# The convolution module of a decoder trunk: where the norm, the output weights and the layer norm stand in the queues

## The chip, the cores and the metric

The kernel runs on one core of one Trainium2 chip. Its engines each work through a queue of their own in order: TensorE (PE) multiplies matrices, VectorE (DVE) and GpSimd (POOL) do elementwise work and reductions, ScalarE (ACT) activations and copies, SyncE (SP) issues most of the transfers. The metric is the device time of one execution in microseconds (us). It is 1263.67 us before, the median of three runs (1261.9 to 1269.88).

## What is computed

Two decoder layers over 512 positions with 1024 channels, in float32. Each layer is a mixer and a SwiGLU feed-forward network, both behind an RMS norm and added to the residual. The mixer of layer 0 is a convolution module, that of layer 1 is sparse attention. What the change names is the convolution module:

```python
def conformer_conv_module(h, w_in, b_in, w_dw, b_dw, ln_g, ln_b, w_out):
    a, g = jnp.split(h @ w_in + b_in, 2, axis=-1)
    u = a * jax.nn.sigmoid(g)
    u = lax.conv_general_dilated(u, w_dw[:, None, :], (1,), padding=[(CONV_WIDTH - 1, 0)], ...) + b_dw
    mu = jnp.mean(u, axis=-1, keepdims=True)
    var = jnp.mean(jnp.square(u - mu), axis=-1, keepdims=True)
    u = (u - mu) * lax.rsqrt(var + LN_EPS) * ln_g + ln_b
    return jax.nn.silu(u) @ w_out
```

Its input h is rmsnorm(x), the convolution runs over 31 positions, each channel for itself. The attention projects h to queries, keys, values and gates; queries and keys are each normalized per head and rotated in part of their channels (rope):

```python
    q = partial_rope(rmsnorm(q, q_gain), positions)
    k = partial_rope(rmsnorm(kv[:, 0], k_gain[:, None, None, None, :]), positions)
```

## The kernel before

All activations lie with channels on the 128 partitions and the 512 positions along them, so x is 8 chunks of 128 x 512. Every product with a weight is made of three matmuls: the weight tile wr is split into a rounded part wh (ScalarE, L198) and the rest wl = wr - wh (VectorE, L207), the input into hh and hl in the same way, and mm3 (L258 to L260) adds wh x hh, wh x hl and wl x hh. Weight tiles come in a fixed sequence: w_dma (L183) issues the load of a tile on SP, next_w (L210) splits a tile, starts the split of the next and loads up to four ahead. proj_tile (L356) makes one 128 x 512 result of 24 matmuls. After its fourth input chunk it splits the next wl and calls `mid`, if one was given. proj_start (L333) makes the first four results of a projection together, chunk by chunk of the input.

The order on each engine is partly set by a scheduler: instructions given to tc.keep_in_program_order keep their place in the written order, `after(a, b)` puts a behind b, and the others are placed by the scheduler. mm3 pins its matmuls only while a flag (`hold`) is set.

The convolution module (L370) goes through these steps. The input projection starts with the raw x, and the norm's scale R comes later: norm_a (L314) sums the squares (ssq) and runs a chain of small operations for the inverse root, norm_b (L323) spreads the scale over all partitions (rbc, eight matmuls) and copies it to Rb. glu(i) (L416) then makes gr and ar (a result times Rb) and u_i from the two results pA and pG of chunk i. A loop (L599) makes pA and pG of chunk i, with glu of chunk i - 1 between them. Chunks 0 and 1 are convolved on VectorE (cv, L438), chunks 2 to 7 on PE: conv_pe_load stores u_i to memory in one layout (swap<-u, L451) and loads it in another (uf<-swap, L452), conv_pe multiplies it with a band matrix (cpe, L471), adds bias terms (L475), stores (swap<-uf, L476) and loads it back (u<-swap, L481). The sums for the layer norm of a PE chunk are the matmuls lng (ph_sum, L519). The table CONV_AT says at which chunk of the loop each of these steps is written down: "c" a convolution, "g" the sums of one, "w" the loads, "n" and "m" the sums of chunks 0 and 1, "t" the spreading of these (lnrt). Three buffers hold uf, so the sixth and later loads wait until an older chunk's sums are done.

ln_rows (L544) makes the two rows rs and mr of the layer norm, spread by lnb. ln_out(i) (L618) normalizes a chunk: a product and a subtraction on VectorE (L621 or L623, L624), two activations (L630) and the low part (L631). proj_start calls it one chunk ahead of the output projection, whose eight chunks need weight tiles wr18 to wr25. Tiles 18 to 20 are loaded in the loop before `at(8)`.

In the attention layer (layer 1), q_tiles (L1410) makes the query results, six of them through proj_tile with `mid` set to a function that runs the steps of the table MIDS and may be empty; the keys' results and the first two of the queries', ahead of them, give no `mid`. Between the tiles stand short pieces of PE work: qk_rs (L997) sums the squares of a group of heads (psq), turns them (qat), takes the inverse root on VectorE, turns it back (qyt) and makes qys through ScalarE (L1018) and VectorE (L1019); qk_norm (L1022) spreads qys over a result's partitions (bc) and multiplies; the rotation takes ScalarE's scaling (L1097), four small transfers (rot<-qraw, L1101), a product on GpSimd (L1107) and two operations on VectorE (L1108, L1109); cmp_mlp (L1172) makes z.

Of the kernel before, what the change touches and what calls it, by code (L numbers as in the profile page):

```python
# [14 lines left out]
AF = mybir.ActivationFunctionType  # L15
ALU = mybir.AluOpType
# [3 lines left out]
P = 128  # L20
# [37 lines left out]
BAND_BUFS = 3  # L58
SPLIT = {7: 2}
EH = 2  # L60
CONV_AT = {4: ("s",), 5: ("c2", "c3"), 6: ("g0", "c4"), 7: ("g1", "g2", "n0", "c5"),
           8: ("w", "n1", "m0", "m1", "c6", "g3", "c7", "t", "g4", "g5")}
NLN = len(LN_ORDER)
PH_B = 48
NPH = PH_B + 8 * len(PE_CONV)
# [43 lines left out]
def trunk(ctx: ExitStack, tc: tile.TileContext, A, out):  # L109
# [51 lines left out]
        add("nw_o", i, 1024)  # L161
    add_ffn(1)

    raws, split, los = {}, {}, set()
    pin = {}

    def after(a, b):
# [15 lines left out]
    def w_dma(i):  # L183
        if i in raws or i >= len(units):
            return
        ap, cols = units[i]
        t = wp.tile([P, 1024], F32, tag="wr", name=f"wr{i}")
        nc.sync.dma_start(t[:, :cols], ap)
        raws[i] = t

    def w_hi(i):
# [54 lines left out]
    def v(col, n=1):  # L246
        return vec[:, col:col + n]
# [82 lines left out]
        nc.scalar.activation(R, ps2, AF.Copy)  # L330
        return R

    def proj_start(pool, tag, xh, xl, hooks=None, pre=None):  # L333

        hooks = hooks or {}
        pss = [pool.tile([P, T], F32, tag=tag, name=nm("pp")) for _ in range(4)]
        if pre:
            pre(0)
        for i in range(4):
            wh, wl = next_w()  # L340
            for k2 in range(2):
                k = 2 * i + k2
                if pre and k + 1 < NK:
                    pre(k + 1)
                for m in range(4):
                    c = slice(k2 * T + m * P, k2 * T + (m + 1) * P)
                    mm3(pss[m], wh[:, c], wl[:, c], xh[k], xl[k], k == 0, k == NK - 1)
                    if (k, m) in hooks:
                        hooks[k, m]()
                if k2 == 0:  # L350
                    w_lo()
                if k in hooks:
                    hooks[k]()
        return pss

    def proj_tile(pool, tag, xh=None, xl=None, mid=None):  # L356
        xh, xl = xh or hh, xl or hl
        ps = pool.tile([P, T], F32, tag=tag, name=nm("pp"))
        wh, wl = next_w()
        for k in range(NK):  # L360
            c = slice(k * P, (k + 1) * P)
            mm3(ps, wh[:, c], wl[:, c], xh[k], xl[k], k == 0, k == NK - 1)
            if k == 3:
                w_lo()
                if mid:
                    mid()
        return ps


    def conv_module():  # L370
        acc = new_acc()
        with ExitStack() as cx:
# [39 lines left out]
            R = norm_b(norm_a(acc, pa, "pa"), pa, "pa")  # L412

            last = {}

            def glu(i, pA, pG):  # L416
                gr = ct.tile([P, T], F32, tag="A", bufs=3, name=f"gr{i}")
# [29 lines left out]
            def conv_pe_load(i):  # L447
                f = cp.tile([P, 8, 68], F32, tag="uf", bufs=3, name=f"uf{i}")
                nc.gpsimd.memset(f[:, :, :4], 0.0)
                chan, phase = views()  # L450
                nc.sync.dma_start(chan, u[i][:, 32:].rearrange("p (r t) -> p r t", r=8))  # L451
                nc.sync.dma_start(f[:, :, 4:], phase)  # L452
                return f

            def conv_pe(j, i, f):
# [25 lines left out]
                nc.sync.dma_start(vt[i], chan)  # L481
                sh["g", i] = ce, nb, n

            sh = {}
# [1 line left out]
            def by_phase(z):  # L486

                return z.rearrange("p (t r) -> p r t", r=8)
# [108 lines left out]
                        conv_pe(PE_CONV.index(c), c, ups[c])  # L597

            for i in range(1, NK):  # L599
                pA = proj_tile(pm, "pm")  # L600
                glu(i - 1, *pend)
                after_glu(i - 1)
                pG = proj_tile(pm, "pm")
                pend = (pA, pG)
                at(i)
            glu(NK - 1, *pend)
# [1 line left out]
            state["end"] = len(units)  # L608
            for k in range(18, 21):
                w_dma(k)  # L610
            at(8)
            rs, mr = ln_rows()
            px.close()

            po = cx.enter_context(tc.tile_pool(name="po", bufs=6, space=PSUM, reuse_waits="tile"))
            ah, al = [], []

            def ln_out(i):  # L618
                if i in PE_CONV:
                    vch[i] = cp.tile([P, T], F32, tag="c", bufs=2, name=f"c{i}")  # L620
                    nc.vector.tensor_tensor(by_phase(vch[i]), vt[i], by_phase(rs), ALU.mult)  # L621
                else:
                    nc.vector.tensor_tensor(vch[i], vch[i], rs, ALU.mult)  # L623
                nc.vector.tensor_tensor(vch[i], vch[i], mr, ALU.subtract)  # L624
                y = ct.tile([P, T], F32, tag="A", bufs=3, name=f"lny{i}")
                if i == 0:
                    box["a"] = [cp.tile([P, NK, T], F32R, tag="bd", bufs=BAND_BUFS, name=f"a{s}") for s in range(2)]
                h_, l_ = (z[:, i, :] for z in box["a"])
                for z in (h_, y):
                    nc.scalar.activation(z, vch[i], AF.Silu, scale=v(V_LNG + i), bias=v(V_LNB + i))  # L630
# [1143 lines left out]
```

## Time and profile before

| what | value |
| --- | --- |
| time, median of 3 runs | 1263.67 us (1261.9 to 1269.88) |
| span of the profiled execution | 1259.1 us |
| PE busy | 1224.2 us, 97% |
| VectorE busy | 810.1 us, 64% |
| ScalarE busy | 567.2 us, 45% |
| GpSimd busy | 339.5 us, 27% |
| convolution module up to the first output matmul | 0 to 153.2 us |
| query and key phase of the attention | 620 to 700 us |

The profiled execution's span, from its first to its last instruction, is 1259.1 us; the median of the timed runs is 4.6 us above that. In the rows of the timeline the first number is the start in us, the second the duration; "x3" counts instructions, and the bracket tells how long the engine was idle before and what released it. In a row of the waits stand the total, the number of times and the longest. In a row of the windows stand the bounds, the length, then busy time and instructions of PE, PE's weight loads, VectorE, ScalarE and GpSimd, and last the granted clock of PE, the share of the DMA engines and GB/s.

### The profile page before, as it was taken

How to read it: one execution, taken by the hardware profiler on the slowest of the kernel's cores; microseconds unless marked ns; L12 is line 12 of the kernel's file. 1: busy time of each engine (PE TensorE's matmuls, PEld its weight loads, DVE VectorE, ACT ScalarE, POOL GpSimd, SP SyncE). 2: the span in 40 equal slices, each digit the busy share in tenths (PEclk: the TensorE clock that was granted, in tenths of full speed). 3: DMA queues.
4: the chain of work that ended last, by engine and by line, in shares of the span. 5: the costliest groups of instructions: out<-in, count | busy, mean ns of one | idle time of the engine just before them, and what ended most of it. 6: DMA issues, size and time to landing. Idle time of an engine off the chain costs nothing.

```text
span 1259.1 us, 20754 instructions
## 1 busy us (share of the span) xinstructions
PE 1224.2 (97%) x8015; PEld 1034.0 (82%) x8015; DVE 810.1 (64%) x1455; ACT 567.2 (45%) x1046; POOL 339.5 (27%) x395
## 2 busy tenths in 40 slices
PE   9999799999999999999998999999999999999998
PEld 6787588799999988887777776667878999998886
DVE  6996486978766645335687787753497766656221
ACT  5222263455555533223444677773354555544111
POOL 2011022135443001131432465651303544410000
PEclk9999999999999999999999899999999999999999
DMA  8758426347776132244256101001523877722331
GB/s 309 262 164 306 100 84 185 117 118 192 205 189 160 54 106 93 92 150 125 61 140 166 25 18 43 1 18 51 184 100 109 199 193 193 180 79 101 109 112 43
DMA packets 82115, 161.62 MB, mean 128 GB/s; under 512 B 36064, under 2 KB 36960, under 8 KB 80480
## 3 DMA queue, kind: packets, MB, share of 16 engines
q1 hardware_dynamic: 65808, 108.54, 27.0%
q0 software_dynamic: 16208, 51.75, 16.3%
q8 instruction: 63, 1.03, 0.3%
q14 instruction: 36, 0.29, 0.1%
HBM read 146.73 MB, written 5.28 MB: 121 GB/s over the span
## 4 chain that ended last, share of the span: by engine, by line
PE 78%; DVE 8%; DMA 4%; issue 3%; SPq 3%; ACT 2%; POOL 1%; DVEq 0%; POOLq 0%; ACTq 0%
PE st L780 27%; PE pp L258 7%; PE pp L260 7%; PE pp L259 7%; PE st L260 7%; PE st L258 7%; PE st L259 7%; PE O L1516 3%; PE cpe L471 2%; DVE Pm L1462 1%; PE T L1490 1%; PE S L1459 1%; SPq L1101 1%; DVE t L1493 1%; DMA rot<-qraw 1%
## 5 line engine op out<-in xcount | busy, mean ns | idle before, releaser
L198 ACT ACTIVATE wh<-wr 128x1024 fp32r<-128x1024 f32 (+3 forms) x158 | 160.4, 1015 | 315.1 <-PE st L259 143.3
L207 DVE TENSOR_TENSOR wl<-wr,wh 128x1024 fp32r<-128x1024 f32 (+3 forms) x158 | 190.7, 1207 | 124.8 <-ACT wh L198 121.3
L780 PE MATMUL st<-bh,sl 128*128 128x256 f32 x680 | 192.6, 283 | 1.1 <-DVE sl L764 1.1
L780 PE MATMUL st<-bh,sh 128*128 128x256 f32 x680 | 192.8, 284 | 0.0
L780 PE MATMUL st<-bl,sh 128*128 128x256 f32 x680 | 192.0, 282 | 0.0
L258 PE MATMUL pp<-hh,wh 128*128 128x512 f32 x416 | 165.4, 400 | 3.1 <-DVE gr L418 1.9
L260 PE MATMUL pp<-hh,wl 128*128 128x512 f32 x416 | 164.7, 398 | 1.0 <-DVE wl L207 0.9
L259 PE MATMUL pp<-hl,wh 128*128 128x512 f32 x416 | 165.2, 398 | 0.0
L260 PE MATMUL st<-ah,wl 128*128 128x512 f32 x352 | 139.6, 396 | 0.0
L258 PE MATMUL st<-ah,wh 128*128 128x512 f32 x352 | 139.5, 396 | 0.0
L259 PE MATMUL st<-al,wh 128*128 128x512 f32 x352 | 139.5, 396 | 0.0
L780 PEld LDWEIGHTS st<-bh,sl 128*128 128x128 f32 x680 | 130.2, 191 | 1.5 <-DVE sl L764 1.5
L780 PEld LDWEIGHTS st<-bl,sh 128*128 128x128 f32 x680 | 130.6, 192 | 0.1
L780 PEld LDWEIGHTS st<-bh,sh 128*128 128x128 f32 x680 | 130.0, 191 | 0.1
L764 DVE TENSOR_TENSOR sl<-S,sh 128x512 fp32r<-128x512 f32 x136 | 94.2, 734 | 40.7 <-ACT sh L763 40.4
L258 PEld LDWEIGHTS pp<-hh,wh 128*128 128x128 f32 x416 | 78.9, 190 | 24.3 <-ACT wh L198 3.1
L1477 POOL TENSOR_SCALAR Pm<-Pm,sm,gates 128x512 f32<-128x512 f32 (+3 forms) x128 | 80.8, 644 | 63.6 <-DVE sm L1473 52.9
L260 PEld LDWEIGHTS pp<-hh,wl 128*128 128x128 f32 x416 | 78.5, 189 | 21.0 <-DVE wl L207 2.9
L259 PEld LDWEIGHTS pp<-hl,wh 128*128 128x128 f32 x416 | 78.7, 189 | 18.9 <-issue 1.1
L754 POOL TENSOR_TENSOR S<-S,wr 128x512 f32<-128x512 f32 x34 | 49.2, 1448 | 154.6 <-DVE sl L764 82.4
L1463 ACT ACTIVATE Pm<-Pm,mx 128x512 f32<-128x512 f32 (+3 forms) x128 | 71.1, 557 | 37.9 <-DVE mx L1462 35.1
L302 POOL TENSOR_TENSOR acc<-acc,sq 128x512 f32<-128x512 f32 x18 | 31.7, 1761 | 206.8 <-ACT sq L300 193.1
(280 smaller groups left out, 2525.4 us busy)
## 6 DMA issues: line engine op xcount, KB each, us to landing
S<-fw_x POOLq DMA_DIRECT2D x68, 512.0 KB, 5.7
wr<-fw_in SPq DMA_DIRECT2D x46, 512.0 KB
wr<-fw_o SPq DMA_DIRECT2D x32, 512.0 KB
bd<-bands POOLq DMA_DIRECT2D x12, 1280.0 KB, 11.3
r<-fw_x SPq DMA_DIRECT2D x34, 256.0 KB
wr<-cw_in SPq DMA_DIRECT2D x14, 512.0 KB
wr<-fw_o SPq DMA_DIRECT2D x16, 384.0 KB
wr<-fw_s SPq DMA_DIRECT2D x8, 512.0 KB
```

The lines of the kernel that those rows point to most:

```text
L198: parted(after(nc.scalar.activation(hi[:, :cols], raws[i][:, :cols], AF.Copy), pin.get(AF)))
L207: parted(after(nc.vector.tensor_tensor(lo[:, :cols], raws[i][:, :cols], hi[:, :cols], ALU.subtract), pin.get(ALU)))
L258: held(nc.tensor.matmul(ps, wh, xh, start=first, stop=False))
L259: held(nc.tensor.matmul(ps, wh, xl, start=False, stop=False))
L260: held(nc.tensor.matmul(ps, wl, xh, start=False, stop=last))
L302: (eng or nc.gpsimd).tensor_tensor(acc, acc, sq, ALU.add)
L754: pe(nc.gpsimd.tensor_tensor(t[:, :T], S[n][:, :T], w[:, :T], ALU.add))
L764: pe(nc.vector.tensor_tensor(l_[:, c], z, h_[:, c], ALU.subtract))
L780: pe(nc.tensor.matmul(ps[:, :H], p_[:, k], m_[c][:, t], start=first and c == 0 and q == 0, stop=last and c == 3 and q == 2, skip_group_che ...
L1463: at_[AF] = nc.scalar.activation(Pt, Pt, AF.Exp, bias=mx, scale=-1.0, accum_out=sm)
L1477: nc.gpsimd.tensor_scalar(Pt, Pt, sm[:, k:k + 1], gates[:, t + k, br * 16 + h:br * 16 + h + 1], ALU.mult, ALU.mult)
L1516: pe(nc.tensor.matmul(o[par * 64:par * 64 + 64, P * kc:], vf[br][:, kc, g], Us[par][kc], start=False, stop=last))
```

## The change

The matmuls of proj_tile are pinned one by one where `mid` is given, and the first pair of tiles of the convolution now gives one: norm_1 (ssq and the inverse root) in the middle of pA1, norm_2 (rbc, Rb and the glu of chunk 0) in the middle of pG1. CONV_AT moves the sums g1 ahead of the convolution of chunk 4 and the step "t" ahead of g3 and the convolution of chunk 7. The loads of weight tiles 18 to 20 are put behind the last uf load, those from 21 on behind the last load back. ln_out is pinned by engine in its written order, its low part one chunk later, and the output projection's start does the low products of a chunk last.

```diff
-CONV_AT = {4: ("s",), 5: ("c2", "c3"), 6: ("g0", "c4"), 7: ("g1", "g2", "n0", "c5"),
-           8: ("w", "n1", "m0", "m1", "c6", "g3", "c7", "t", "g4", "g5")}
+CONV_AT = {4: ("s",), 5: ("c2", "c3"), 6: ("g0", "g1", "c4"), 7: ("g2", "n0", "c5"),
+           8: ("w", "n1", "m0", "m1", "c6", "t", "g3", "c7", "g4", "g5")}
...
-        nc.sync.dma_start(t[:, :cols], ap)
+        raw_dma[i] = after(nc.sync.dma_start(t[:, :cols], ap), state.get("behind"))
...
+                    if low_last:
+                        first, last = k == 0, k == NK - 1
+                        kept = tc.keep_in_program_order
+                        kept(nc.tensor.matmul(pss[m], wh[:, c], xh[k], start=first, stop=False))
+                        kept(nc.tensor.matmul(pss[m], wl[:, c], xh[k], start=False, stop=False))
+                        if m < 3:
+                            continue
+                        for n in range(4):
+                            c = slice(k2 * T + n * P, k2 * T + (n + 1) * P)
+                            kept(nc.tensor.matmul(pss[n], wh[:, c], xl[k], start=False, stop=last))
+                        continue
...
-            mm3(ps, wh[:, c], wl[:, c], xh[k], xl[k], k == 0, k == NK - 1)
+            if mid:
+                kept = tc.keep_in_program_order
+                kept(nc.tensor.matmul(ps, wh[:, c], xh[k], start=k == 0, stop=False))
+                kept(nc.tensor.matmul(ps, wh[:, c], xl[k], start=False, stop=False))
+                kept(nc.tensor.matmul(ps, wl[:, c], xh[k], start=False, stop=k == NK - 1))
+            else:
+                mm3(ps, wh[:, c], wl[:, c], xh[k], xl[k], k == 0, k == NK - 1)
...
-                pA = proj_tile(pm, "pm")
-                glu(i - 1, *pend)
-                after_glu(i - 1)
-                pG = proj_tile(pm, "pm")
+                pA = proj_tile(pm, "pm", mid=norm_1 if i == 1 else None)
...
+                def norm_2():
+                    nonlocal R
+                    R = norm_b(last["r"], pa, "pa")
+                    gated()
...
+                pG = proj_tile(pm, "pm", mid=norm_2 if i == 1 else None)
...
             for k in range(18, 21):
                 w_dma(k)
+                after(raw_dma[k], last["load"])
             at(8)
+            state["behind"] = last["back"]
...
-                nc.vector.tensor_tensor(vch[i], vch[i], mr, ALU.subtract)
+                kept(nc.vector.tensor_tensor(vch[i], vch[i], mr, ALU.subtract))
...
-                nc.vector.tensor_tensor(l_, y, h_, ALU.subtract)
+                box[i] = h_, l_, y
...
+                if i:
+                    ln_low(i - 1)
+                if i == NK - 1:
+                    ln_low(i)
...
-            pss = proj_start(po, "po", ah, al, pre=ln_out)
+            pss = proj_start(po, "po", ah, al, pre=ln_out, low_last=True)
```

Three places in the queues show what this does. The first is VectorE's queue at chunk 3 of the convolution. pp_37 is the result pA3, and wl9 is the low part of the weight for the tile behind it. Before:

```order
L438 SCALAR_TENSOR_TENSOR cv0_363<-u0_137,wdw_102,cv0_363 128x512
L207 TENSOR_TENSOR wl9_528<-wr9_430,wh9_527 128x1024
L438 SCALAR_TENSOR_TENSOR cv0_363<-u0_137,wdw_102,cv0_363 128x512
L427 SCALAR_TENSOR_TENSOR u2_139<-ar2_560,vec_74,gr2_557 128x64x8
L438 SCALAR_TENSOR_TENSOR cv0_363<-u0_137,wdw_102,cv0_363 128x512 x2
L421 TENSOR_TENSOR ar3_635<-pp_37_526,Rb_32_323 128x512
```

After:

```order
L446 SCALAR_TENSOR_TENSOR u2_139<-ar2_560,vec_74,gr2_557 128x64x8
L457 SCALAR_TENSOR_TENSOR cv0_382<-u0_137,wdw_102,cv0_382 128x512 x3
L440 TENSOR_TENSOR ar3_635<-pp_37_526,Rb_34_374 128x512
L457 SCALAR_TENSOR_TENSOR cv0_382<-u0_137,wdw_102,cv0_382 128x512
L207 TENSOR_TENSOR wl9_528<-wr9_430,wh9_527 128x1024
```

wl9 has moved from ahead of ar3 to behind it, and ar3 needs the end of the tile ahead.

The second is SP's queue at the last swaps (swap<-u is a store, uf<-swap a load, u<-swap a load back, wr a weight). Before:

```order
L451 DMA swap_54_1141<-u6_143 128x8x64
L476 DMA swap_52_1013<-uf4_721 1024x1x64
L188 DMA wr21_1575<-cw_os 128x1024
L481 DMA u4_141<-swap_52_1013 128x8x64
L452 DMA uf6_1139<-swap_54_1141 128x8x64
L188 DMA wr22_1618<-cw_o 128x1024
L451 DMA swap_57_1272<-u7_144 128x8x64
L476 DMA swap_56_1176<-uf5_976 1024x1x64
L452 DMA uf7_1270<-swap_57_1272 128x8x64
```

After:

```order
L470 DMA swap_54_1143<-u6_143 128x8x64
L471 DMA uf6_1141<-swap_54_1143 128x8x64
L495 DMA swap_52_1015<-uf4_721 1024x1x64
L500 DMA u4_141<-swap_52_1015 128x8x64
L470 DMA swap_57_1272<-u7_144 128x8x64
L471 DMA uf7_1270<-swap_57_1272 128x8x64
L188 DMA wr18_1275<-cw_os 128x1024
L188 DMA wr19_1277<-cw_os 128x1024
L188 DMA wr20_1279<-cw_os 128x1024
```

The weights have left the swaps; wr18 to wr20 stand behind the load of chunk 7, and wr21 and wr22, not shown, behind the last load back. VectorE's splits wl18 and wl19 have moved with them, from between ar7 and u7 to between the additions of uf5 and uf6.

The third is PE's queue in the query phase, at the tiles with the weights 88 and 89 (pp_598 is the tile of weight 89). Before:

```order
L260 MATMUL pp_598_6235<-hh5_509_5291,wl89_6178 128x512
L1024 MATMUL bc_584_6151<-qys_575_6056,er_5520 128x512
L1024 MATMUL bc_585_6154<-qys_575_6056,er_5520 128x512
L1024 MATMUL bc_586_6164<-qys_575_6056,er_5520 128x512
L258 MATMUL pp_598_6235<-hh6_513_5384,wh89_6177 128x512
L259 MATMUL pp_598_6235<-hl6_514_5385,wh89_6177 128x512
L260 MATMUL pp_598_6235<-hh6_513_5384,wl89_6178 128x512
L258 MATMUL pp_598_6235<-hh7_517_5477,wh89_6177 128x512
L259 MATMUL pp_598_6235<-hl7_518_5478,wh89_6177 128x512
L260 MATMUL pp_598_6235<-hh7_517_5477,wl89_6178 128x512
L258 MATMUL pp_616_6377<-hh0_491_4865,wh90_6236 128x512
L1116 MATMUL psq_603_6280<-qsq_597_6228,sel_5517 32x512
```

After, at the same bc (which now stand ahead of the tile of weight 88), and at the same psq:

```order
L377 MATMUL pp_582_6116<-hh7_517_5477,wl87_6071 128x512
L1061 MATMUL qyt_574_6051<-cc_103,qy2_573_6048 64x128 x4
L1070 MATMUL bc_584_6151<-qys_575_6056,er_5520 128x512
L1070 MATMUL bc_585_6154<-qys_575_6056,er_5520 128x512
L1070 MATMUL bc_586_6164<-qys_575_6056,er_5520 128x512
L375 MATMUL pp_589_6176<-hh0_491_4865,wh88_6117 128x512
```

```order
L377 MATMUL pp_598_6235<-hh7_517_5477,wl89_6178 128x512
L1162 MATMUL psq_603_6280<-qsq_597_6228,sel_5517 32x512
L1162 MATMUL psq_603_6280<-qsq_588_6169,sel_5517 32x512
L1162 MATMUL psq_603_6280<-qsq_581_6106,sel_5517 32x512
L1162 MATMUL psq_603_6280<-qsq_577_6062,sel_5517 32x512
L1050 MATMUL qat_606_6291<-sel_5517,qa_605_6289 128x8 x4
L1061 MATMUL qyt_611_6314<-cc_103,qy2_610_6311 64x128 x4
L1223 MATMUL z_613_6323<-kb0_6157,w1_0_5683 64x65 x32
L375 MATMUL pp_616_6377<-hh0_491_4865,wh90_6236 128x512
```

The 24 matmuls of a tile now stand together, and qyt with its bc, and psq with its qat and the next qyt, stand directly behind one another. On VectorE, behind qat, stand 13 small operations up to the copy qy that qyt reads, and four of 128 x 512 among them, the last of which adds the rotation of the tile of weight 89.

More of the change, by code (lines that the diff above doesn't have):

```diff
@@ L162, in trunk @@
     add_ffn(1)
-    raws, split, los = {}, {}, set()
+    raws, raw_dma, split, los = {}, {}, {}, set()
     pin = {}
@@ L331, in norm_b, with proj_start @@
         return R
-    def proj_start(pool, tag, xh, xl, hooks=None, pre=None):
+    def proj_start(pool, tag, xh, xl, hooks=None, pre=None, low_last=False):
         hooks = hooks or {}
@@ L411, in conv_module, with norm_1 @@
                 load_band(n)
-            R = norm_b(norm_a(acc, pa, "pa"), pa, "pa")
+            R = None
             last = {}
+            def norm_1():
+                last["r"] = norm_a(acc, pa, "pa")
             def glu(i, pA, pG):
@@ L451, in conv_pe_load @@
                 nc.sync.dma_start(chan, u[i][:, 32:].rearrange("p (r t) -> p r t", r=8))
-                nc.sync.dma_start(f[:, :, 4:], phase)
+                last["load"] = nc.sync.dma_start(f[:, :, 4:], phase)
                 return f
@@ L480, in conv_pe @@
                 vt[i] = u[i][:, 32:].rearrange("p (r t) -> p r t", r=8)
-                nc.sync.dma_start(vt[i], chan)
+                last["back"] = nc.sync.dma_start(vt[i], chan)
                 sh["g", i] = ce, nb, n
@@ L599, in conv_module, with gated @@
             for i in range(1, NK):
-                pA = proj_tile(pm, "pm")
-                glu(i - 1, *pend)
-                after_glu(i - 1)
-                pG = proj_tile(pm, "pm")
+                pA = proj_tile(pm, "pm", mid=norm_1 if i == 1 else None)
+                def gated():
+                    glu(i - 1, *pend)
+                    after_glu(i - 1)
+                def norm_2():
+                    nonlocal R
+                    R = norm_b(last["r"], pa, "pa")
+                    gated()
+                if i > 1:
+                    gated()
+                pG = proj_tile(pm, "pm", mid=norm_2 if i == 1 else None)
                 pend = (pA, pG)
@@ L616, in conv_module, with kept, ln_low @@
             ah, al = [], []
+            chain = {}
+            def kept(z):
+                chain[z.ins.engine] = after(z, chain.get(z.ins.engine))
+                return z
+            def ln_low(i):
+                h_, l_, y = box[i]
+                kept(nc.vector.tensor_tensor(l_, y, h_, ALU.subtract))
             def ln_out(i):
@@ L620, in ln_out @@
                     vch[i] = cp.tile([P, T], F32, tag="c", bufs=2, name=f"c{i}")
-                    nc.vector.tensor_tensor(by_phase(vch[i]), vt[i], by_phase(rs), ALU.mult)
+                    kept(nc.vector.tensor_tensor(by_phase(vch[i]), vt[i], by_phase(rs), ALU.mult))
                 else:
-                    nc.vector.tensor_tensor(vch[i], vch[i], rs, ALU.mult)
-                nc.vector.tensor_tensor(vch[i], vch[i], mr, ALU.subtract)
+                    kept(nc.vector.tensor_tensor(vch[i], vch[i], rs, ALU.mult))
+                kept(nc.vector.tensor_tensor(vch[i], vch[i], mr, ALU.subtract))
                 y = ct.tile([P, T], F32, tag="A", bufs=3, name=f"lny{i}")
@@ L629, in ln_out @@
                 for z in (h_, y):
-                    nc.scalar.activation(z, vch[i], AF.Silu, scale=v(V_LNG + i), bias=v(V_LNB + i))
-                nc.vector.tensor_tensor(l_, y, h_, ALU.subtract)
+                    kept(nc.scalar.activation(z, vch[i], AF.Silu, scale=v(V_LNG + i), bias=v(V_LNB + i)))
+                box[i] = h_, l_, y
                 ah.append(h_)
                 al.append(l_)
+                if i:
+                    ln_low(i - 1)
+                if i == NK - 1:
+                    ln_low(i)
             box = {}
-            pss = proj_start(po, "po", ah, al, pre=ln_out)
+            pss = proj_start(po, "po", ah, al, pre=ln_out, low_last=True)
+            state["behind"] = None
             acc = new_acc()
```

## The prediction

> **What bounds the kernel now.** I read the page first, then the waits of PE in the stretches that the change touches, then the timeline around each wait.
>
> ```profile
> span 1259.1 us, 20754 instructions
> PE 1224.2 (97%) x8015; PEld 1034.0 (82%) x8015; DVE 810.1 (64%) x1455; ACT 567.2 (45%) x1046; POOL 339.5 (27%) x395
> ```
>
> PE is busy for 1224.2 of 1259.1 us. No edit takes matmuls away, so only PE's idle time, 34.9 us in the whole program, and stretches at a lowered clock can be won. A new wait of PE is paid in full.
>
> ```profile
> PE cpe L471 <- DMA uf<-swap: 3.1, 3, 1.6
> PE pp L258 <- DVE gr L418: 1.9, 1, 1.9
> PE pp L258 <- ACT a L630: 1.8, 1, 1.8
> ```
>
> These are PE's waits between 20 and 160 us, the convolution module (total, count, longest). The three named edits aim at exactly these: the first tiles (1.9), the swaps (3.1) and the layer norm (1.8). Together 6.8 us, 0.5% of the time. The same view between 620 and 700 us, in the attention layer's q and k phase:
>
> ```profile
> PE qyt L1015 <- DVE qy L1011: 2.2, 2, 1.3
> PE bc L1024 <- DVE qys L1019: 1.5, 1, 1.5
> PE pv L1351 <- DVE wl L207: 1.2, 1, 1.2
> ```
>
> This phase is not in the title of the change, but its code calls proj_tile with `mid`, and the diff fixes the order of the matmuls wherever `mid` is given. That is the part I weigh most.
>
> **A. Norm inside the first two tiles.** Before, the norm's scale came after the second tile; PE waited the 1.9 us above for gr, and then ran slowly:
>
> ```profile
> 33.64 0.63 PE L260 MATMUL pp<-hh,wl 128*128 128x512 f32 x1
> 34.07 0.63 PE L258 MATMUL pp<-hh,wh 128*128 128x512 f32 x1
> ```
> ```profile
> 34.00:60.00 26.00, 26.00 (x107) 20.82 (x106) 24.18 (x33) 6.21 (x7) 0.00 (x0) 0.95 0.68 249
> ```
>
> These matmuls start 0.43 us apart, and the row of the window, whose last three numbers are granted clock, DMA share and GB/s, has a clock of 0.95 over 26 us: 0.05 x 26 = 1.3 us lost. With the scale ready half a tile earlier both go: -1.9 - 1.3 = -3.2. Against this, VectorE is busy for 24.18 of those 26 us, and wl9 now stands behind ar3 and one cv (order fence of the first place). The PE tile pG3 starts when ar3 may start, so wl9 is ready after one wide operation, one cv and one weight split: with about 0.65 us from start to start of wide operations (the VectorE rows of D) and 1.2 for a weight split (the page's mean of its group), about 2.5 us. PE has four matmuls that don't need it, about 0.22 each at full clock (half of 0.43), 0.9. That is a new wait of about 1.5 (0 if VectorE has caught up by then, which nothing in a row excludes; 2.5 at most). **A = -1.7**, between -3.2 and -0.7.
>
> **B. The swaps.** The queue of SP, before:
>
> ```profile
> 111.00 6.01 SPq L188 DMA_DIRECT2D wr<-cw_os  x1
> 117.07 1.97 SPq L451 DMA_DIRECT2D swap<-u  x1
> ...
> 125.35 0.58 SPq L452 DMA_DIRECT2D uf<-swap  x1
> 126.04 0.65 SPq L188 DMA_DIRECT2D wr<-cw_o  x1
> 126.80 0.37 SPq L451 DMA_DIRECT2D swap<-u  x1
> ...
> 132.59 0.57 SPq L452 DMA_DIRECT2D uf<-swap  x1
> ```
> ```profile
> 135.99 5.41 PE L471 MATMUL cpe<-uf,bd 128*64 128x64 f32 x160 [1.13 <-DMA uf<-swap]
> ```
>
> A weight load held the queue from 111.00 to 117.01, and the store of chunk 6 stood behind it; another weight load stood between chunk 6's load (125.35) and chunk 7's store, and chunk 7's load came at 132.59. Each load lands a few us later and PE waits: 3.1 in all. In the change these stores and loads stand in one piece without a weight, and the early g1 frees chunk 6's buffer one tile sooner. I take the whole -3.1 (0 if the transfers themselves, not the queue, are late). What is late next: wl18 and wl19 stand on VectorE ahead of the uf6 addition. Their weights are issued behind chunk 7's load. Chunk 7's 256 KB took 3.4 us from issue (132.59) to PE's start on them (135.99). If its load is now issued near 126 and two weights of 512 KB behind it land in 3.4 to 7 us, the two splits of 1.2 end between 132 and 136, while PE ends chunk 6 some 3 us earlier than before; uf6's addition waits 0 to 3 us. PE needs that only where chunk 7 runs out of result buffers, so I price it at +0.7. The earlier lnrt moves 0.9 us of matmuls to where PE works anyway: nothing either way. **B = -2.4** (-3.1 to +1).
>
> **C. Layer norm by chunk.**
>
> ```profile
> 148.54 1.29 DVE L623 TENSOR_TENSOR u<-u,lnb 128x512 f32<-128x512 f32 x2 [1.05 <-PE lnb L566]
> 149.75 1.99 DVE L621 TENSOR_TENSOR c<-u,lnb 128x512 f32<-128x512 f32 x2
> 151.58 1.27 DVE L624 TENSOR_TENSOR u<-u,lnb 128x512 f32<-128x512 f32 x2
> ```
> ```profile
> 152.29 0.81 ACT L630 ACTIVATE a<-u,vec 128x512 fp32r<-128x512 f32 x1 [8.92 <-DVE u L624]
> ```
>
> Four products stood ahead of chunk 0's subtraction. ScalarE's first activation, for which PE waits, starts at 152.29. By chunk, product and subtraction are done by 148.54 + 0.65 + 0.65 = 149.85, and ScalarE starts there: -2.4. The low products stand behind eight matmuls (1.8 us) and have that long. After that a chunk costs VectorE 1.0 + 0.65 + 0.65 = 2.3 us against PE's twelve matmuls, 2.6, so no later chunk waits. **C = -2.4** (-3 to -2). A + B + C = **-6.5**, bounds -9.3 to -1.7.
>
> **D. The pinned q tiles.** The six tiles of q_tiles are now whole blocks in PE's queue, and short matmuls that hang on one another stand bare between them.
>
> ```profile
> 625.94 0.69 DVE L1137 TENSOR_TENSOR qraw<-pp,Rb 128x512 f32<-128x512 f32 x1
> 626.59 0.69 DVE L1108 TENSOR_TENSOR qraw<-qraw,cosT 128x512 f32<-128x512 f32 x1
> 627.20 2.33 DVE L207 TENSOR_TENSOR wl<-wr,wh 128x1024 fp32r<-128x1024 f32 x1
> 629.45 0.68 DVE L1109 TENSOR_TENSOR qraw<-qraw,t 128x512 f32<-128x512 f32 x1
> ```
> ```profile
> 626.25 0.60 PE L1015 MATMUL qyt<-cc,qy 128*64 128x128 f32 x4
> ...
> 635.82 1.07 PE L1116 MATMUL psq<-qsq,sel 128*32 128x512 f32 x8
> ...
> 644.66 1.03 PE L1004 MATMUL qat<-sel,qa 128*128 128x8 f32 x8
> ```
>
> Before, psq and qat were 9 us apart, with projection matmuls between, and so were the other pairs. First wait: bc needs qys on VectorE, behind one qraw, one cosT product and one split. With the durations of these rows qys takes the place of 629.45, ends at 630.1, and qyt ended at 626.85: 3.3 us idle (1.5 if VectorE were free, the bc row of the waits above; 4). Second: psq to qat through ScalarE's copy (636.96):
>
> ```profile
> 634.72 0.72 ACT L1097 ACTIVATE qraw<-qraw,vec 128x512 f32<-128x512 f32 x1
> 635.47 1.06 ACT L198 ACTIVATE wh<-wr 128x1024 fp32r<-128x1024 f32 x1
> 636.96 0.60 ACT L1001 ACTIVATE qa<-psq 128x512 f32<-128x512 f32 x1 [0.43 <-PE psq L1116]
> ```
> ```profile
> 640.43 1.81 POOL L1107 TENSOR_TENSOR t<-rot,sinT 128x512 f32<-128x512 f32 x1 [4.20 <-DMA rot<-qraw]
> ```
>
> 0.8 us (0.7 to 2). Third, and largest: qat to qyt. Thirteen small operations on VectorE, 0.2 us each as an estimate (they are 128x32), are 2.6 us, and the four wide ones among them 2.6. The last wide one adds a rotation of the tile just projected. That path is: evacuation on VectorE 0.7; ScalarE's copy, square and scaling, 0.6 + 0.6 + 0.7; the rotating transfers; GpSimd's product 1.81; the addition 0.7. From the scaling's end (635.44) to the product (640.43) the rows show 5.0 us; with an empty queue I take 2. From the tile's end that is 7.1 to 10.1 us, of which psq, copy and qat fill 1.07 + 0.8 + 1.03 = 2.9: 4.2 to 7.2 idle. I take 6.0, nearer the upper end, which a row shows (2.6 if only the small chain counted). New waits: 3.3 + 0.8 + 6.0 = **+10.1**. Waits that go: one of the two of qyt, 0.9 (2.2 less 1.3), the late bc's 1.5, since that bc now stands among other matmuls, and half of 1.2: **-3.0**. VectorE and the transfers gain 7 to 10 us of lead on PE there, so I add no others.
>
> The clock also moves:
>
> ```profile
> 685.00:690.00 5.00, 2.27 (x18) 1.80 (x16) 3.11 (x6) 1.75 (x3) 2.22 (x6) 1.00 0.64 179
> 690.00:695.00 5.00, 4.59 (x21) 3.79 (x21) 3.91 (x9) 1.34 (x4) 0.00 (x0) 0.71 0.48 147
> 695.00:700.00 5.00, 5.00 (x26) 4.91 (x27) 2.56 (x9) 1.80 (x6) 2.19 (x4) 0.60 0.02 5
> ```
>
> 2.7 us idle between 685 and 690 are followed by clocks of 0.71 and 0.60: 0.29 x 5 + 0.40 x 5 = 3.4 us lost. A's stall cost 1.3. Two new stalls of over 3 us at 1.7 each are +3.4; the old loss goes at even odds, -1.7. Clock **+1.7** (-3.4 to +5). **D = 10.1 - 3.0 + 1.7 = +8.8**, bounds +3 to +16.
>
> [...]
>
> **Sum.** 1259.1 - 6.5 + 8.8 = 1261.4 us of span. The median of the runs shown, 1263.67, lies 4.6 us above the span, so the forecast is **1266 us**, no change that can be told.
>
> **Rivals.** (1) D is hidden, because the code before and after has the same dependences and the q phase was waiting anyway (qyt 2.2, bc 1.5). Then A, B and C are what is left: 1263.7 - 6.5 = 1257. Against it: in the order of the change nothing stands between qat and qyt. (2) The bare chain costs its upper bounds: 4 + 2 + 7.2, only 1.5 of old waits vanish, two clock losses of 3.4 us with none won back, and the convolution gives only 3: 1263.7 + 11.7 + 6.8 - 3 = 1279. Slower by over 1% begins where D exceeds the gain by 12.6. The place is PE between the last matmul with wl89 and the first with wh90; for it speaks the rotation path of up to 10.1 us, against it that the old waits behind it had the same causes and would then go. (3) The tail does not get what it is meant to: chunk 7's load is late all the same, or the two splits hold uf6 so long that B is +1: 1266 + 3.4 = 1269. For it: the DMA share is part of each landing time, which the order cannot change. (4) The first tiles' gain is mostly eaten by wl9, A = -0.7: 1267, inside the forecast.
>
> **How the numbers follow.** Forecast with (3) and (4): 0.65. D hidden or small (1): 0.18. Upper bounds (2): 0.17. What can be told from no change is about 1%, 12.6 us: below 1251 or above 1276. Faster needs A to C at their bounds, D at nothing (1263.7 - 9.3 = 1254) and the old clock loss back: 0.05, all from (1). Slower: three quarters of (2), 0.13. Same: 0.82. The range takes in (1) with some spread and ends just short of (2): 1255 to 1278.
>
> **What would show it.** In the profile of the change: PE's wait for gr near 33 and for uf near 121 to 136 gone; the first out-projection matmul 2 us or more earlier against lnb; a wait for wl near 49; and in the q phase two waits, bc on qys of about 3 and qyt on qy of about 6, with half-clock matmuls behind. The forecast is wrong if these two waits are under 2 us together, or if the convolution ends less than 3 us earlier.

## The result, and the profile after

The change takes 1276.84 us (median of four runs, 1275.78 to 1278.86) against 1263.67 before: a ratio of 1.0115, 95% interval 1.0079 to 1.0151. It is slower by 13 us. The forecast was 1266 and no change that can be told.

Read in the same order as before, the page of the change first:

```profile
span 1277.1 us, 20745 instructions
PE 1226.3 (96%) x8015; PEld 1037.2 (81%) x8015; DVE 810.0 (63%) x1455; ACT 567.7 (44%) x1046; POOL 338.0 (26%) x395
```

PE does the same work (1226.3 us busy, 1224.2 before) in a span 18.0 us longer; what was added is 15.9 us of idle time and 2.1 us of longer matmuls. The two profiled executions lie further apart than the medians (18.0 against 13.2): single executions of one kernel scatter by some us (28 of the 29 of the kernel before that stand beside e13 to e15 took 1253.35 to 1266.99), so the differences in the table below are checked against the other kernels' profiles further on. The waits of PE up to 180 us, then those between 560 and 760 us:

```profile
PE cpe L490 <- DVE uf L494: 5.8, 1, 5.8
PE cpe L490 <- DMA uf<-swap: 4.0, 2, 2.4
PE pp L258 <- ACT wh L198: 1.8, 3, 0.7
PE pp L260 <- DVE wl L207: 1.6, 2, 0.9
```
```profile
PE qyt L1061 <- DVE qy L1057: 15.9, 3, 8.1
PE bc L1070 <- DVE qys L1065: 3.2, 1, 3.2
...
PE qat L1050 <- ACT qa L1047: 0.7, 1, 0.7
```

The waits for gr (1.9) and for the layer norm's a (1.8) are gone. At the swaps, which were to be freed, PE waits 9.8 us in place of 3.1, and 5.8 of that is a wait that did not exist before: for VectorE. In the query phase stand the waits that the forecast looked for, and more of them.

Four stretches, each between two marks in the profile, tell the parts apart: A from the first matmul of the input projection to the last gr, B from there to the layer norm's sums (lnpt), C from the rows of the layer norm (lnb) to the first state of the feed-forward network, D from the first z of the keys to the first matmul O<-t of the attention.

| stretch, us | before | change | difference | forecast |
| --- | --- | --- | --- | --- |
| A first tiles | 114.65 | 112.73 | -1.9 | -1.7 |
| B swaps | 23.84 | 32.44 | +8.6 | -2.4 |
| C layer norm | 111.1 | 108.4 | -2.7 | -2.4 |
| D query phase | 119.2 | 133.4 | +14.2 | +8.8 |
| sum | | | +18.2 | +2.3 |

So A and C came as forecast, D had the right sign and place and was too small, and B has the wrong sign.

One profiled execution below, that of e1, was disturbed behind the convolution (span 4042 us), so only its convolution is read.

### The profile page after: what moved, and what is told of

Read it like the earlier page. It is cut to its first block, busy times and chain, and to the rows that moved or that the text cites. A ratio compares the mean times of both kernels' runs of the same rounds, so it can differ in the third digit from the quotient of the medians.

```text
span 1277.1 us, 20745 instructions
## 1 busy us (share of the span) xinstructions
PE 1226.3 (96%) x8015; PEld 1037.2 (81%) x8015; DVE 810.0 (63%) x1455; ACT 567.7 (44%) x1046; POOL 338.0 (26%) x395
## 4 chain that ended last, share of the span: by engine, by line
PE 71%; issue 11%; DVE 9%; DMA 3%; ACT 2%; POOL 2%; SPq 1%; DVEq 0%; POOLq 0%; ACTq 0%
PE st L826 26%; PE st L260 6%; PE st L258 6%; PE st L259 6%; PE pp L258 4%; PE pp L260 4%; PE pp L259 4%; PE O L1562 3%; DVE Pm L1508 1%; PE T L1536 1%; PE cpe L490 1%; PE S L1505 1%; DVE cv L457 1%; PE pv L1397 1%; DMA uf<-swap 1%
## 5 line engine op out<-in xcount | busy, mean ns | idle before, releaser
L258 PE MATMUL pp<-hh,wh 128*128 128x512 f32 x352 | 139.8, 400 | 2.8 <-ACT wh L198 2.7
L260 PE MATMUL pp<-hh,wl 128*128 128x512 f32 x352 | 138.4, 396 | 1.6 <-DVE wl L207 1.6
L259 PE MATMUL pp<-hl,wh 128*128 128x512 f32 x352 | 138.8, 396 | 0.0
L258 PEld LDWEIGHTS pp<-hh,wh 128*128 128x128 f32 x352 | 66.1, 188 | 21.5 <-ACT wh L198 5.0
L260 PEld LDWEIGHTS pp<-hh,wl 128*128 128x128 f32 x352 | 66.1, 188 | 17.9 <-DVE wl L207 2.7
L809 ACT ACTIVATE sh<-S 128x512 fp32r<-128x512 f32 x136 | 78.1, 619 | 3.4 <-POOL S L800 3.4
```

The costliest lines, as they stand in the source:

```text
L258: held(nc.tensor.matmul(ps, wh, xh, start=first, stop=False))
L259: held(nc.tensor.matmul(ps, wh, xl, start=False, stop=False))
L260: held(nc.tensor.matmul(ps, wl, xh, start=False, stop=last))
L809: pe(nc.scalar.activation(h_[:, c], z, AF.Copy))
```

## The experiments

The ratio of each kernel is to runs of the kernel before on the same chip, with its 95% interval. The marks of A to D are read from each kernel's profiled execution.

**Undoing the two suspects, and the pins alone.** Three kernels undo a part of the change, the fourth does one part on the kernel before.

```diff
# e1, in the change: pins only in the convolution's pool
-            if mid:
+            if mid and tag == "pm":
# e2, in the change: weights where they were
-                after(raw_dma[k], last["load"])
-            state["behind"] = last["back"]
# e3: both edits
# e4, in the kernel before: the pinned branch of proj_tile, nothing else
```

> The change, with the matmuls of a tile pinned only in the convolution's pool; the query tiles are left to the scheduler as before. Theory one (the pinned query tiles lay chained short matmuls bare): the query phase's waits for qy and qys, 15.9 and 3.2 us in the change, fall back to about the 3.7 of before, and the half-clock stretches there go: 14 us less than the change's 1276.8, 1263 (1260 to 1266). Theory two (PE would have waited there anyway, the pins only say where): less than 6 us come back, 1271 or more.

> The change, with the output weights loaded where they were before (no place behind the last swaps); the other parts stay. Theory one (the splits wl18 and wl19 stand on VectorE ahead of the addition of chunk 6 and wait for weights that now come late): the wait of cpe for uf on VectorE, 5.8 us, goes, and the half clock behind it: 8 us less than the change, 1269 (1266 to 1271). Theory two (the swaps' transfers are late by themselves, whichever queue they stand in): the waits for uf stay near 10 us in sum, 1274 or more.

> Both of the foregoing: the change without the pinned query tiles and with the output weights where they were. Theory one: the two costs add, since they lie 480 us apart: 1276.8 - 14 - 8 = 1255, faster than before by what the first tiles, the sums' order and the layer norm give (5 to 8 us). Theory two: 1266 or more.

> The kernel before, and only the pinning of the matmuls of a tile where mid is given, so of the six query tiles. Theory one: 14 us more than before, 1277 (1274 to 1280), with the same waits in the query phase as the change (qy about 16, qys about 3). Theory two: the pins cost less than 6, 1269 or less, and the rest of the loss comes from another part.

Measured: e1 1.0017 (0.9997 to 1.0038), e2 1.008 (1.0051 to 1.0109), e3 0.9997 (0.9975 to 1.002), e4 1.0085 (1.0048 to 1.0123). The pins alone on the kernel before cost 10.7 us, and taking them out of the change returns 12.4. Stretch D is 133.4, 133.8 and 131.8 us in the change, e2 and e4, all with the pins, and 117.9 to 121.9 (mean 120.1) in the twelve profiles without them: 12.9 us. Theory one holds for the query tiles, and theory two (PE would have waited anyway) falls.

For the weights the result is less clear: by the medians e2 is 4 us under the change, with intervals that overlap, where 8 were expected, and e3 equals the kernel before, where 1255 was expected. The wait for VectorE is gone in both, but the wait for transfers is not, 3.9 and 5.8 us, and stretch B is 24.5 and 27.6 us against 22.5 to 24.4 (mean 23.4) in the five profiles that have the queue of before there. So the moved sums seem to cost 1 to 4 us of their own, which was in neither theory. It is not shown: e2 and e3 have the same convolution and lie 3 us apart.

**Splits late, another queue, the two good parts alone, and the clock.**

```diff
# e5 = e1, the first splits of the output weights behind chunk 7's last addition and square
+            pin.update({AF: last["sq"], ALU: last["add"]})
             pss = proj_start(po, "po", ah, al, pre=ln_out, low_last=True)
+            pin.clear()
# e6 = e3, chunk 7's store and load on ScalarE's queue
+                q = nc.scalar if i == 7 else nc.sync
# e7 = e3 with CONV_AT of before
# e8 = the change, and in qk_rs ahead of the turns of qyt
+            warm(py, (18, 34, 14)[len(rsn) - 1], z)
```

> The first experiment's kernel (query tiles free), the output weights still loaded behind the swaps, but the splits of weights 18 and 19 put behind the last addition of chunk 7 on VectorE and behind the last square on ScalarE. Theory one (the order on VectorE makes the wait): the wait of cpe for uf on VectorE, 4.0 us there, and the half clock behind it go; from the end of the input projection to the layer norm's sums 25 us in place of 31, and 5 us less than that kernel's 1.0017 of before: 0.998. Theory two (the swaps' own transfers set the end): chunk 7 waits for its load in place of VectorE, 30 us, 1.001.

> The third experiment's kernel (query tiles free, weights where they were), with the store and the load of chunk 7 issued by ScalarE's queue. If SP's order makes chunk 7 late (its store stands behind a return that waits for another transfer), its wait for the load, 3.3 and 3.7 us in the last two profiles, goes: 3 us less than that kernel, 0.997 of before. If the transfers themselves are slow, nothing changes: 1.000.

> The change with free query tiles, the weights where they were and the table of the convolution as before: what is left is the norm inside the first two tiles and the layer norm by chunk. By the profiles so far the layer norm gives 2.7 us and the first tiles about 1.1 (less than the forecast 1.7): 0.997 of before, 1259.5. If the moved sums were a gain, this is slower than the third experiment's kernel; by its tail (26 us against 23 in the order of before) it is faster by 2 to 3.

> The change with 18, 34 and 14 matmuls of zeros in bfloat16 (about 0.21 us each) written into the tile of qyt ahead of its three turns, which overwrite it; they fill about the time that PE waits there. The waits end when VectorE and GpSimd end, so they don't get shorter. Theory one (part of the query phase's cost is the half clock behind the waits): 3 to 5 us less than the change, 1272 to 1274. Theory two (the half clock costs nothing, as the work behind waits for others anyway): 1 us at most.

Measured: e5 1.0014 (0.9992 to 1.0036), e6 0.9963 (0.9944 to 0.9982), e7 0.9978 (0.9955 to 1.0), e8 1.0091 (1.0062 to 1.012).

e5 shortens B from the 31.2 us of e1 to 26.6, and no wait for VectorE is left, so the order on VectorE did make that wait (4.0 us in e1). But its time is that of e1 within the intervals. Most of the gain is given back one step later: the splits now stand among the layer norm's small operations.

```profile
144.03 1.21 DVE L207 TENSOR_TENSOR wl<-wr,wh 128x1024 fp32r<-128x1024 f32 x1
145.16 0.15 DVE L572 TENSOR_TENSOR st<-st,lnpt 128x8 f32<-128x8 f32 x1
145.23 1.22 DVE L207 TENSOR_TENSOR wl<-wr,wh 128x1024 fp32r<-128x1024 f32 x1
146.37 0.15 DVE L575 SCALAR_TENSOR_TENSOR var<-st 128x4 f32<-128x4 f32 x1
```

PE's wait for rsy, between B and C, rises from 1.2 to 2.9 us, the clock is 0.86 between 150 and 160, and C is 110.0 in place of 108.4: together 3.3 of the 4.6 us. A split of 1.2 us is cheap only where nobody waits.

e6 and e7 come as expected within their intervals; e6 is faster than both kernels. Its chunk 7 still waits 1.1 us for its load, so the queue's order was a part of that wait and not all. e7 is e3 with the sums where they were; it is 2 us faster, with intervals that overlap, which points to a cost of the moved sums and does not show it.

e8 asks what the clock costs. The same stretch, in the change and in e8 (length, PE busy, granted clock, DMA share, GB/s):

```profile
650.00:655.00 5.00, 1.49 (x13) 0.76 0.77 205
655.00:660.00 5.00, 0.00 (x0) 0.50 0.72 191
660.00:665.00 5.00, 4.71 (x69) 0.50 0.27 70
```
```profile
650.00:655.00 5.00, 5.00 (x25) 1.00 0.83 216
655.00:660.00 5.00, 4.35 (x60) 1.00 0.83 222
660.00:665.00 5.00, 5.00 (x44) 1.00 0.26 56
```

In D of e8, PE is idle for 7.1 us and busy with zeros for 14.7, together 22 us, against 21 us idle in the change: it is about as far from useful work as before. But its clock stays up (1.00 from 640 to 720 us, 0.91 from 620 to 640), the 701 useful matmuls take 107.9 us in place of 112.2, and D falls from 133.0 (the mean with pins) to 128.5, in one profile. By the medians the gain is 3.0 us (1.0115 against 1.0091, whose intervals overlap). The test is not clean: of the zeros only the 34 stand in the wait, the 18 were placed inside the tile ahead and the 14 right behind qat, and 18 of the z moved ahead of the second qyt.

These 4.5 us are not a part of the 12.9 that the pins cost, for the kernels without pins lose clock in D too:

| stretch D, mean of | length | PE idle | PE busy | granted clock |
| --- | --- | --- | --- | --- |
| three profiles with pins | 133.0 | 21.0 | 112.0 | 0.90 |
| twelve without | 120.1 | 9.1 | 111.0 | 0.96 |

So 12 of the 12.9 us are waits, and 1 us is matmuls at a lower clock.

**Each part by itself, and a sum of the good ones.**

```diff
# e9, in the kernel before: only the weights behind the swaps
+                after(raw_dma[k], last["load"])
+            state["behind"] = last["back"]
# e10: only the layer norm by chunk; e11: only the norm inside the first tiles
# e12 = e7, chunk 7's store and load on ScalarE's queue
```

> The kernel before, and only the loads of the output weights behind the swaps (18 to 20 behind the last load of a chunk, the rest behind the last load back). Theory one (the splits of 18 and 19 then block VectorE ahead of chunk 6's addition): a wait of cpe for uf on VectorE of 4 to 6 us that the kernel before does not have, a tail of 30 to 33 us from the last gr to the layer norm's sums in place of 22.5 to 24, 4 to 8 us slower than before, 1.003 to 1.006. Theory two (that wait comes from the moved sums together with the weights): no such wait, 1.000.

> The kernel before, and only the layer norm by chunk with the low products last. By the stretch from lnb to the first feed-forward state, 111.1 us before and 108.3 to 108.4 in the profiles of the change: 2.7 us less, 0.998. If the earlier start is given back later, 1.000.

> The kernel before, and only the norm inside the first two tiles (with their matmuls pinned). Forecast: the wait for gr and the half clock go, 3.2 us, a new wait for wl near 50 takes 1.5: 1.7 us less. By the profiles so far (111.5 to 113.8 from the first matmul to the last gr, before 113.2 and 114.7) it is about 1.4: 0.999.

> The norm inside the first tiles, the layer norm by chunk, the convolution's table and the weights as before, the query tiles free, and the store and the load of chunk 7 issued by ScalarE. If the three gains add (1.4, 2.7 and 2 to 3 for chunk 7): 6 to 7 us less than before, 0.995. If chunk 7's own queue helps only with the moved sums of the sixth experiment's kernel: 0.997.

Measured: e9 1.001 (0.9992 to 1.0029), e10 0.9979 (0.9956 to 1.0001), e11 0.9987 (0.9967 to 1.0008), e12 0.9964 (0.9946 to 0.9983). The layer norm gives its 2.7 us in C every time (108.3 or 108.4 in all profiles that have it but e5's). The first tiles are at the edge of what can be told: A is 112.7 on the mean of thirteen profiles with the edit and 113.8 on the mean of four without, 1.1 us, but e9, without the edit, has 112.1. By its ratio e12 gained less than the sum (0.995, which its interval holds): chunk 6, whose load is not on the other queue, waited 3.1 us there.

e9 was the surprise. Its waits between 100 and 150 us:

```profile
PE cpe L471 <- DVE uf L475: 2.7, 1, 2.7
PE lnb L566 <- DVE rsy L277: 1.2, 1, 1.2
PE lnpt L550 <- DVE red L547: 1.0, 1, 1.0
```

Not one wait for a transfer is left: with the weights out of the queue the 3.1 us are won (1.3 to 3.2 in the five profiles with the queue of before), as the forecast's term had it. The wait for VectorE takes their place (2.7, priced at 0.7), and B is 24.3, no change that can be told. So in B, against the mean of 23.4, weights alone cost about 1 us, moved sums alone 1 to 4, and both together 8 to 10. That they don't add was the open question.

**What joins them.** The queue of SP in the change:

```profile
109.22 0.58 SPq L471 DMA_DIRECT2D uf<-swap  x1
109.85 0.69 SPq L470 DMA_DIRECT2D swap<-u  x1
121.44 0.58 SPq L471 DMA_DIRECT2D uf<-swap  x1
122.06 0.67 SPq L495 DMA_DIRECT2D swap<-uf  x1
127.18 0.37 SPq L500 DMA_DIRECT2D u<-swap  x1
127.67 0.50 SPq L470 DMA_DIRECT2D swap<-u  x1
```

Chunk 6's store is issued at 109.85 and its load at 121.44, as soon as the store has landed. The queue stands for 11 us at that load. Behind it stand chunk 4's store and its load back (which waits for that store) and chunk 7's store, though u7 was done at 120.7. The front part shows the rows: before, chunk 4's store and load back stood ahead of chunk 6's load. Three buffers hold uf, so from the fourth load on (the front part says the sixth) each waits for an older chunk's sums; chunk 6's, the fifth, needs chunk 3's, which are g1. The early g1 frees that buffer early, and so the load is put ahead.

GpSimd's queue at the same time, in the change and in e13 below, which has g1 as before:

```profile
108.80 0.12 POOL L468 MEMSET uf<- 128x32 f32 x1 [2.79 <-DMA swap<-uf]
108.88 1.04 POOL L478 TENSOR_TENSOR nb<-ph,sp 128x512 f32<-128x512 f32 x1
109.86 1.09 POOL L410 DMA_DIRECT2D bd<-bands  x2
```
```profile
107.00 1.09 POOL L410 DMA_DIRECT2D bd<-bands  x2 [1.17 <-PE cpe L490]
119.17 0.12 POOL L468 MEMSET uf<- 128x32 f32 x1 [11.08 <-PE lng L547]
```

Two band transfers of 1280 KB run beside chunk 6's store, and in all eight profiles with the early g1 the store lands 0.7 to 1.0 us behind the second of them (120.33 and 121.31 in the change). With the early g1 the freed buffer is cleared ahead of the bands' issue, so they start later too, at 109.86 in place of 107.00. The place of the load in SP's queue and the later bands both come with the early g1, and no run parts them.

Two kernels put back one moved step each; a third leaves the sums as before and puts the splits where PE does not wait.

```diff
# e13 = e1 with g1 as before
-    6: ("g0", "g1", "c4"), 7: ("g2", "n0", "c5")
+    6: ("g0", "c4"), 7: ("g1", "g2", "n0", "c5")
# e14 = e1 with "t" as before
# e15 = e1 with CONV_AT of before, the splits pinned behind chunk 6's addition and square
```

> The first experiment's kernel (query tiles free, weights behind the swaps), with the sums g1 where they were; the early lnrt stays. Theory three (the early g1 frees a buffer, so that chunk 6's load stands on SP ahead of chunk 4's store and return, and holds these and chunk 7's store until chunk 6's own store has landed behind the band transfers): chunk 7's load is issued near 125 in place of 132, no wait of cpe for a transfer over 1 us there, a tail of 24 to 25 us as with the weights alone (24.3) in place of 31 to 32, 0.997 of before. Theory four (the early lnrt or the weights do it): 31 us, 1.002.

> The first experiment's kernel with the step lnrt where it was; the early g1 stays. Theory three: nothing changes, a tail of 31 to 32 us and 1.002 of before. Theory four: the tail falls to 25, 0.997.

> The norm in the first tiles, the layer norm by chunk, the weights behind the swaps, the table of the convolution as before, query tiles free, and the splits of weights 18 and 19 put behind the addition and the square of chunk 6. By theories one and three no wait for uf is left, neither for a transfer (the weights alone had none) nor for VectorE (2.7 with half a clock behind it): a tail of 21 us, 7 us less than before in all, 0.994 to 0.995. If the splits then hold chunk 7's additions instead: 0.997.

Measured: e13 0.9995 (0.9971 to 1.0019) with B of 25.2 us, e14 1.0047 (1.0023 to 1.007) with B of 33.3, e15 0.9959 (0.9938 to 0.998) with B of 22.1. The queue of e13:

```profile
110.02 5.82 SPq L470 DMA_DIRECT2D swap<-u  x1
115.94 1.07 SPq L495 DMA_DIRECT2D swap<-uf  x1
119.75 0.36 SPq L500 DMA_DIRECT2D u<-swap  x1
120.22 0.58 SPq L471 DMA_DIRECT2D uf<-swap  x1
121.27 0.36 SPq L470 DMA_DIRECT2D swap<-u  x1
125.62 0.58 SPq L471 DMA_DIRECT2D uf<-swap  x1
```

Chunk 7's store goes out at 121.27 in place of 127.67, its load at 125.62 in place of 131.97 (134.00 in e14), and no wait for a transfer is left. Theory four falls: the early g1 and not the early lnrt made the tail long. Theory three holds by its marks; how much of the 8 us in B is the place in the queue and how much the later bands stays open. By the medians e13 is 6 us under e14, and their intervals do not overlap. e13's time is higher than expected (0.997); its wait for VectorE of 3.6 us is still there. e15 has neither wait:

```profile
PE cpe L490 <- issue: 1.4, 1, 1.4
PE lnb L589 <- DVE rsy L277: 1.2, 1, 1.2
PE lnpt L573 <- DVE red L570: 1.0, 1, 1.0
PE cpe L490 <- DMA uf<-swap: 0.3, 1, 0.3
```

With a span of 1254.3 us and 5.2 us less by its ratio it is, with e6 and e12 (whose intervals overlap its own), one of the versions that beat both kernels.

## Why the prediction was wrong, point by point

The four terms missed by 15.9 us together (+2.3 forecast, +18.2 measured): B by 11.0 and D by 5.4, while A and C came 0.5 better. That 1276.84 lies inside the stated range, near its top, is luck: by the working that end belonged to large waits in D alone.

**The waits of PE decide, since it is 97% busy.** Right: the added 18.2 us of the four stretches are the added 18.0 of the span, and 15.9 of these are idle time.

**A, -1.7.** Right in mechanism, -1.9 in the first pair and -1.1 on the mean. The wait for gr and the slow matmuls behind it are gone (the clock is 1.00 from 34 to 60 us, where it was 0.95). The new wait for wl is 0.9 where 1.5 was taken; another of 0.5, for wh on ScalarE, was not in the working, and that the two make up the 1.5 is luck.

**C, -2.4.** Right: -2.7, also alone. The first output matmul starts 3.7 us after the first lnb in place of 5.8.

**B, -2.4, is the step that failed**, at two places. "I take the whole -3.1" took the early g1 as a help ("frees chunk 6's buffer one tile sooner"). The order rows showed chunk 6's load ahead of chunk 4's store, and the question that the working asks elsewhere, what is queued behind the waiting instruction, was not asked here: a load that waits 11 us for its store's landing holds everything behind it. Chunk 7's load, priced as issued "near 126", went out at 131.97, no sooner than before (132.59). e13, which has all of the change's convolution but the early g1, issues it at 125.62 and has B of 25.2, where the change, e1 and e14 have 31.2 to 33.3. And "uf6's addition waits 0 to 3 us ... so I price it at +0.7": the wait was 5.8 in the change, 2.7 to 4.1 in e1, e9, e13 and e14, and PE paid it in full, since chunk 7's blocks stopped for result buffers. VectorE in the change:

```profile
125.62 0.69 DVE L494 TENSOR_TENSOR uf<-cpe,nb 128x512 f32<-128x512 f32 x1 [4.41 <-PE cpe L490]
137.91 1.23 DVE L207 TENSOR_TENSOR wl<-wr,wh 128x1024 fp32r<-128x1024 f32 x1 [11.59 <-ACT wh L198]
140.68 1.23 DVE L207 TENSOR_TENSOR wl<-wr,wh 128x1024 fp32r<-128x1024 f32 x1 [1.54 <-ACT wh L198]
141.82 0.68 DVE L494 TENSOR_TENSOR uf<-cpe,nb 128x512 f32<-128x512 f32 x1
```

The second split ends at 141.9 and not between 132 and 136, because chunk 7's load, behind which its weight is loaded, went out at 131.97 and not near 126. The first error fed the second; but in e13 the splits end at 135.7, as worked out, and PE still waits 3.6 us, so the +0.7 was too low by itself. In and behind the idle time the granted clock fell, from 1.00 (130 to 135 us) to 0.72 (135 to 140) and 0.50 (140 to 145), with 0.76 from 145 to 150, a cost that the sum of B did not have at all. The row at 0.50 (length, PE busy, granted clock, DMA share, GB/s):

```profile
140.00:145.00 5.00, 2.44 (x46) 0.50 0.32 75
```

Of the 8.6 us of B, 6.6 are idle time of PE (10.8 against 4.2) and 2.0 are longer matmuls (the same 480 cpe take 17.1 against 15.1); the mean clock in B is 0.84 in the change and 1.00 before.

**D, +8.8, was right in place and too small** (+14.2 in this pair, 12.9 on the means; its bounds were +3 to +16). Two of its three new waits came as worked out: bc on qys 3.2 (forecast 3.3), qat on qa 0.7 (0.8). The third, qy, was 8.1 where 6.0 was taken, and by another path: the rotation was done in time, but VectorE began the chain only 1.7 us after qat, behind a split of 2.29 us, and the chain with its wide operations took 6.3.

```profile
650.49 1.78 POOL L1153 TENSOR_TENSOR t<-rot,sinT 128x512 f32<-128x512 f32 x1 [5.98 <-DMA rot<-qraw]
651.06 2.29 DVE L207 TENSOR_TENSOR wl<-wr,wh 128x1024 fp32r<-128x1024 f32 x1
...
653.88 0.18 DVE L1052 TENSOR_SCALAR qb<-qat 128x32 f32<-128x32 f32 x1
...
656.67 1.26 POOL L1153 TENSOR_TENSOR t<-rot,sinT 128x512 f32<-128x512 f32 x1 [4.40 <-DVE kl L1215]
656.73 1.25 DVE L276 TENSOR_TENSOR rst<-rst,qb 128x32 f32<-128x32 f32 x1
...
660.29 1.03 PE L1061 MATMUL qyt<-cc,qy 128*64 128x128 f32 x4 [8.08 <-DVE qy L1057]
```

In the working the rotation's transfers take 2 us with an empty queue; that was an estimate that no row shows, and the shortest stretch in the kernel before, from the end of a scaling (662.58) to its product (666.75), is 4.2. The split and one small operation took 1.1 us more than most of their kind (1.2 and 0.19), each while a product of GpSimd ran; the working of this wait has neither. A fourth wait was left out: the first qyt stood 16 matmuls earlier than before, ahead of the end of a chain on GpSimd, and waited 4.3. Of the old waits 7.1 us went in place of 3.0, the last qyt's grew from 1.3 to 3.5. In sum the waits rose by 11.7 us where 7.1 was forecast, and that is the part of D that was too small. The clock's net cost is the rest, 2.5 us in this pair and 1.0 on the means, against 1.7.

**The rivals.** Rival (2) had the time (1279) and the sign of the result, with +18.5 in D (11.7 of waits and 6.8 of clock) and the convolution gaining 3 us; measured are +14.2 in D and a convolution that cost 4, so its time came close by two errors of opposite sign. Rival (3) named the place of B's failure but capped it at +1. No case put both together.

**The signs.** Gone as forecast is the wait for gr, and the first output matmul comes 2.1 us earlier against lnb. The wait for wl near 49 came, shorter, and so did both waits of the query phase. The waits for uf did not go. The convolution was to end at least 3 us earlier; its first output matmul starts at 157.6 in place of 153.2, and that sign of being wrong stood in the prediction.

**The clock.** It fell at each of the four long gaps. Around those of 4.3 and 3.2 us it was 0.87 from 625 to 630 us, 0.50 from 630 to 635 and 0.60 from 635 to 640. At the gap of 8.1 it was 0.76, 0.50 and 0.50 in the three stretches of 5 us from 650 on, and 0.87 from 665 to 670; at the one of 3.5 it was 0.88 and 0.78 between 700 and 710. The 1.7 us for each new stall was an estimate between the 1.3 and the 3.4 that the rows before gave for two stretches; no run shows the cost of one stall by itself. With the clock at 1.00 from 640 to 720 us, D was 4.5 us shorter in the profile of e8, but the kernels without pins lose clock there as well.

## What to carry to other kernels

Where an edit puts instructions into a fixed order, look for every caller of the function: a parameter that was only a hook became a pin for six tiles of another layer, and that cost 11 to 13 us. When a buffer comes free earlier, ask where its load moves to in an in-order queue, and what then stands behind its wait. A weight that is loaded later also makes its split late; price the split where it stands in the queue of its engine, at the landing of its weight and not at its own 1.2 us.

## What the runs showed of the hardware that was not expected

With matmuls on zeros where the change waits 8.1 us, the granted clock was 1.00 (650 to 660 us in e8, 0.50 to 0.76 in the change), and stretch D was 4.5 us shorter in that profile, although they did no useful work; the medians do not tell the two kernels apart.

A store of 256 KB beside two band transfers of 1280 KB was not landed until 11 us after its issue (109.85 to 121.44), against 4.4 us for chunk 7's (121.27 to 125.62 in e13), which had no such company. In all eight profiles with the early g1 it landed 0.7 to 1.0 us behind the second band transfer. Whether the issue blocked for 5.8 us (110.02, e13) or was done at once (109.85, the change), chunk 6's load went out at 120.2 and 121.4; why the one issue was long and the other short was not tried.
